# Ranking the norms between sublayers in the scheduler's order, in a decoder layer on one core

## The chip, the cores and the metric

The kernel runs on one core of a Trainium2 chip. The metric is the device time of one execution in microseconds (us). PE is the matrix engine, DVE the vector engine, ACT the scalar engine, POOL GpSimd, and SP the engine whose queue issues most of the transfers.

## The reference, cut to what matters

One decoder layer on x of 512 tokens by 1024 channels in float32. Three sublayers follow each other, and each one is wrapped in two RMS norms, one ahead of it and one behind it:

```python
h = h + 0.5 * rmsnorm(swiglu(rmsnorm(h, ffn1_pre_w), ffn1_w_gu, ffn1_w_down), ffn1_post_w)
u = rmsnorm(h, mix_pre_w)
y = token_mixing(u, mem, w_in, ...)      # HGRN2, dilated attention, attention into memory; gated, then w_out
h = h + rmsnorm(y, mix_post_w)
h = h + 0.5 * rmsnorm(swiglu(rmsnorm(h, ffn2_pre_w), ffn2_w_gu, ffn2_w_down), ffn2_post_w)

def rmsnorm(x, w):
    return x * rsqrt(mean(x * x, axis=-1) + 1e-6) * w
```

The two places where a sublayer's last product, its post norm, the sum into h and the next sublayer's pre norm follow each other are called passages here: passage 1 from the first feed-forward net to the mixing, passage 2 from the mixing to the second net. What follows the last product of the second net is called the tail.

## The kernel before, in words

Every float32 product is made of three products of numbers split into a high and a low part (`split`: ACT rounds the high part, DVE subtracts it from the source; `wsplit` does so for weights). Large products go in pairs of 7 products of quarters (`pair`, `product`), which need sums of quarters of the activations: the tiles t1, t2, t3, t4, made at the end of `prenorm`.

The 512 tokens are four tiles of 128, t = 0 to 3. At the end of `ffn`, a loop over t makes two halves of 512 channels with `down` (12 matmuls a half; the last half of t=3 in two pieces of 256, so that what follows can begin sooner). DVE adds each half from PSUM into y, ACT squares it and sums the squares (`square`, L174), DVE multiplies y by the norm's weights in place, DVE and POOL make the factor r (`rstd`: v on DVE, L180, the power on POOL, L181), and `postnorm` adds y times r to h (L244). `out_proj` does the same with its two halves in two outer rounds, so that only the second one has a norm behind it.

Then `after(h, t)` spills h to DRAM and starts `prenorm` as a task: squares, rstd and the scaled halves u (L190) at once, then, when the planner's clock has gone on by `LAT['norm']` = 8 us, two sets of four transposes on PE (L352) into a bank of the pool px (3 banks), the split into xhi and xlo, and a copy to SBUF (`keep`, L208). For t = 2 and 3 the sums of quarters follow in the same task. The planner only decides where in the written program a task's next part stands; its clock goes on by fixed amounts per matmul.

The written program is then put in order by a scheduler at build time. Each instruction has a number, by its place in the program. For each engine the scheduler issues, among the instructions that it takes to be ready by its own estimate of durations, the one with the lowest number. On the chip each engine then goes through its list in that order, and waits on semaphores for what is not there yet. Tiles of a pool with one tag are given out in the order in which the program writes them first, whatever the numbers. The pool `slots` has 37 tiles of 128x512, and holds y, h, gains, u, scratch of the squares, copies and activations alike. Transfers made with `fetch` stay in written order on SP.

In the program behind the passages stand, at passage 1, `values` for the columns C_HI (weights from `rows`, products of all four t), then the pairs of the first HGRN heads; at passage 2, two plain blocks of the second net (`gu_plain`, first for t = 0 and 1, then for t = 2 and 3; their weights come from `wcol`), then pairs.

Of the kernel before, what the change touches and what calls it, by code (L numbers as in the profile page):

```python
# [1 line left out]

# [10 lines left out]
ALU = mybir.AluOpType  # L13
# [6 lines left out]
NT = T // P  # L20
# [24 lines left out]
CHUNKS2 = (2, 4, 4, 4, 4, 4)  # L45

LAT = dict(comb=1.0, mem0=0.5, mem1=8.0, mem2=1.5, hg=1.5, hgx=6.0, hg1=6.0, hg2=11.0, hg3=6.0, hg4=6.0, dil0=4.0, dil1=17.0, dil2=5.0,
           dil3=3.0, norm=8.0, mnorm=5.0, mload=10.0, start=0.1, step=2.0, keep=2.0)
PLAN = dict(early1=2, plain1=2, early2=2, plain2=2)
HALVES = (slice(0, 512), slice(512, 1024))  # L50


class Layer:
# [3 lines left out]
    def __init__(self, ctx, tc):  # L57
# [30 lines left out]

        self.strict = False

    def spawn(self, gen):
        task = [0.0, gen, False]
        self.tasks.append(task)
        self.advance(task)
        return task

    def advance(self, task):  # L100
        outer, self.polling = self.polling, True
        try:
            task[0] = self.t + next(task[1])
        except StopIteration:
            task[2] = True
            self.tasks.remove(task)
        self.polling = outer

    def tick(self, us):
        self.t += us  # L110
        while not self.polling:
            due = [x for x in self.tasks if x[0] <= self.t]
            if not due:
                break
            self.advance(min(due, key=lambda x: x[0]))
# [83 lines left out]
    def prenorm(self, src, gain, t, lat, raw):  # L199


        nc = self.nc
        ts = slice(t * P, (t + 1) * P)
        pts = []

        def keep(hf):
            raw[t, hf] = self.slot((P, 4, P))
            nc.scalar.copy(raw[t, hf], pts[hf])  # L208

        wait = self.strict and t < 2  # L210
        for x in self.normed(src, gain, lat, self.psum if self.strict and t == 1 else self.paux):
            if isinstance(x, float):
                yield x
                continue
            hf = len(pts)
            pts.append(x)
            self.split(self.xhi[hf][:, :, ts], self.xlo[hf][:, :, ts], x)
            if not wait and (t < 2 or hf == 0):
                keep(hf)
        if wait:  # L220
            def later():
                yield LAT['keep']
                keep(0)
                keep(1)
            self.spawn(later())
        if t < 2:
            return
        ts = slice((t - 2) * P, (t - 1) * P)
        x11, x21, x12 = raw[t - 2, 0], raw[t - 2, 1], raw[t, 0]
        t1, t2, t3 = self.slot((P, 4, P)), self.slot((P, 4, P)), self.slot((P, 4, P))  # L230
        self.tt(t1, x11, x12, ALU.subtract)
        nc.vector.scalar_tensor_tensor(out=t2, in0=t1, scalar=-1.0, in1=pts[1], op0=ALU.mult, op1=ALU.subtract)
        self.tt(t3, x12, pts[1], ALU.subtract)
        for n, x in (("t1", t1), ("t2", t2), ("t3", t3)):
            self.split(self.xc[n][0][:, :, ts], self.xc[n][1][:, :, ts], x)
            yield LAT['comb']
        self.tt(t3, x21, t2, ALU.add)
        self.split(self.xc["t4"][0][:, :, ts], self.xc["t4"][1][:, :, ts], t3)
# [127 lines left out]
    def pair(self, ops):  # L366


        nc = self.nc
        a, cp, cq = self.psum((P, HT)), self.slot(), self.slot()  # L370
        self.product(a, ops, 1)
        nc.scalar.copy(cp[:, :HT], a)
        u, v, p7 = cq[:, :HT], cp[:, HT:], cq[:, HT:]
        b = self.psum((P, HT))
        self.product(b, ops, 6)
        self.tt(u, cp[:, :HT], b, ALU.add)
        c = self.psum((P, HT))
        self.product(c, ops, 5)
        nc.scalar.copy(v, c)  # L379
        d = self.psum((P, HT))  # L380
        self.product(d, ops, 7)
        nc.scalar.copy(p7, d)  # L382
        self.tt(v, p7, v, ALU.subtract)
        self.product(a, ops, 2, False)
        self.product(c, ops, 3, False)
        self.product(d, ops, 4, False)
        return a, u, c, d, v
# [30 lines left out]
            self.mm3(out, (x[k][0][:, ts], x[k][1][:, ts]), w[k], k == 0, k == n - 1)  # L418


    def ffn(self, w_gu, w_down, w_post, ready, reload, after, chunks, early, plain):


        nc = self.nc
        y = [[self.slot() for _ in range(2)] for _ in range(NT)]
# [18 lines left out]
        def gu_plain(w, act, cs):  # L444
            n = cs.stop - cs.start
            pg, pu = self.psum((P, n)), self.psum((P, n))
            self.proj_T(pg, w[0], self.uT, cs)
            self.proj_T(pu, w[1], self.uT, cs)
            sg = self.slot((P, n))
            nc.scalar.activation(sg, pg, AF.Silu)  # L450
            self.tt(sg, sg, pu, ALU.mult)
            self.split(act[0][:, cs], act[1][:, cs], sg)
# [17 lines left out]
        tasks, heads = [ready[0]()], []  # L470
# [10 lines left out]
        for i in range(2):  # L481
            self.need(*tasks[i])
            for w, act in heads:
                gu_plain(w, act, slice(i * HT, (i + 1) * HT))
        f0, before, ws = 0, None, []
        for n in chunks:
            act = []
# [22 lines left out]
        h = reload()  # L510
        gain = self.bcast_gain(w_post)
        tasks = []
        for t in range(NT):
            whole, parts = slice(0, 512), (slice(0, 256), slice(256, 512))
            ss = []
            for hf in range(2):
                for cs in parts if hf == 1 and t == NT - 1 else (whole,):
                    down(t, hf, act, [w[hf] for w in ws], False, self.psum, cs)
                    ss.append(self.square(y[t][hf][:, cs], hf, 0.5))
                    if len(ss) == 3:  # L520
                        self.tt(ss[1], ss[0], ss[1], ALU.add)
                        del ss[0]
            self.tt(y[t][0], y[t][0], gain[0], ALU.mult)
            r = self.rstd(ss, 0.5)
            self.tt(y[t][1], y[t][1], gain[1], ALU.mult)
            self.postnorm(r, y[t], h[t], parts if t == NT - 1 else (whole,))
            tasks.append(self.spawn(after(h, t)))
        return tasks


# [448 lines left out]
    def out_proj(self, z, w_out, w_post, reload, after):  # L979

        nc = self.nc
        y, ss = [[None, None] for _ in range(NT)], [[None, None] for _ in range(NT)]
        tasks = []
        gain = self.bcast_gain(w_post)
        for hf in range(2):
            w = self.rows(w_out, hf * 512, 512)
            if hf == 1:
                h = reload()
            for t in range(NT):
                ps = self.psum()  # L990
                self.proj_N(ps, z, slice(t * P, (t + 1) * P), w)
                ss[t][hf] = self.square(ps, hf, 1.0)
                y[t][hf] = self.slot()
                self.tt(y[t][hf], ps, gain[hf], ALU.mult)
                if hf == 1:
                    self.postnorm(self.rstd(ss[t], 1.0), y[t], h[t])
                    tasks.append(self.spawn(after(h, t)))
        return tasks


# [7 lines left out]
def layer_kernel(ctx, tc, a, nbias, hmask, out):  # L1008
    nc = tc.nc
    L = Layer(ctx, tc)  # L1010
    x = a["x"][0]

    gpre, raw = [], {}
# [27 lines left out]
    def spill(name):  # L1041
        return [[L.dram.tile([P, T], F32, tag=f"{name}{t}{hf}", name=f"{name}{t}{hf}") for hf in range(2)] for t in range(NT)]

    def reload(src):
        def go():
            h = [[L.slot() for _ in range(2)] for _ in range(NT)]
            for t in range(NT):
                for hf in range(2):
                    L.fetch(h[t][hf], src(t, hf))
            return h  # L1050
        return go
# [13 lines left out]
    def store(h, t):  # L1065
        for c, n in ((0, 512), (512, 256), (768, 256)) if t == NT - 1 else ((0, 512), (512, 512)):
# [3 lines left out]
    h1, h2 = spill("h1"), spill("h2")  # L1070
    ready = L.ffn(a["ffn1_w_gu"][0], a["ffn1_w_down"][0], a["ffn1_post_w"][0], [first, second],
                  reload(lambda t, hf: x[t * P:(t + 1) * P, HALVES[hf]]), follow(h1, a["mix_pre_w"][0]), CHUNKS1, PLAN['early1'], PLAN['plain1'])
    z = L.mixing(a, ready, nbias)
    ready = L.out_proj(z, a["w_out"][0], a["mix_post_w"][0], reload(lambda t, hf: h1[t][hf]), follow(h2, a["ffn2_pre_w"][0]))
    L.ffn(a["ffn2_w_gu"][0], a["ffn2_w_down"][0], a["ffn2_post_w"][0], [lambda: ready[:2], lambda: ready[2:]], reload(lambda t, hf: h2[t][hf]), store, CHUNKS2, PLAN['early2'], PLAN['plain2'])


def constants():
# [39 lines left out]
```

## Time and profile before

| | us |
|---|---|
| median of 3 runs | 1367.82 (1366.94 to 1368.05) |
| the profiled execution's own time | 1367.62 |
| its span, first to last instruction | 1365.8 |
| PE busy in the span | 1331.6 |
| DVE busy | 1050.7 |
| ACT busy | 742.2 |
| POOL busy | 107.0 |

The span is 1.82 us shorter than the execution's time. A row of the timeline has the start, the duration, the engine, the line, what is written from what, the number of instructions that were merged, and in brackets the idle time of the engine before it with what ended it. A duration includes some overlap with the next instruction of the same engine: DVE rows of 0.68 us stand 0.60 us apart, matmuls of 512 columns (0.39 us) 0.227 us apart, and those of 256 columns (0.28 us) 0.12 us apart. Passage 1 lies at about 345 to 400 us, passage 2 at 980 to 1030 us, the tail from 1335 us on.

### The profile page before, as it was taken

What the parts mean: (1) busy time and instruction counts of PE and PEld (TensorE: products, weight loads), DVE (VectorE), ACT (ScalarE), POOL (GpSimd) and SP (SyncE); (2) the same over time, 40 slices, a digit from 0 to 9 for tenths busy, and PEclk for the clock granted to TensorE, in tenths of its full rate; (3) what the DMA queues carried; (4) which work ended last, traced back from release to release, by engine and by line L of the source; (5) the groups of instructions that cost most, each with busy time, mean ns of one, the idle gap of its engine ahead of it and who ended that gap; (6) DMA issues with size and microseconds to landing.
All of it is one profiled execution on the core that took longest, in us unless ns stands there. A gap on an engine that the chain in (4) does not pass through costs nothing.

```text
span 1365.8 us, 24324 instructions
## 1 busy us (share of the span) xinstructions
PE 1331.6 (97%) x9197; PEld 1233.0 (90%) x9197; DVE 1050.7 (77%) x1996; ACT 742.2 (54%) x1527; POOL 107.0 (8%) x140
## 2 busy tenths in 40 slices
PE   6999999999999999999999999999999999999997
PEld 6999999999789888899899999999889999999996
DVE  6887776777798975598888988897478877677765
ACT  6665544555467655355554755566366655445541
POOL 1111111110100000000000100000011111111100
PEclk9999999999999999999999999999999999999999
DMA  9676565554435335334224333335465765655513
GB/s 271 141 182 184 148 156 142 143 151 125 168 94 177 96 98 163 123 102 117 63 78 124 100 95 93 108 94 154 135 190 135 186 181 151 152 139 148 146 47 139
DMA packets 238123, 185.76 MB, mean 136 GB/s; under 512 B 9109, under 2 KB 198966, under 8 KB 238006
## 3 DMA queue, kind: packets, MB, share of 16 engines
q1 hardware_dynamic: 224246, 160.02, 39.5%
q0 software_dynamic: 12032, 21.04, 9.4%
q10 hardware_dynamic: 1728, 3.15, 0.6%
q8 instruction: 72, 1.18, 0.3%
q14 instruction: 45, 0.37, 0.1%
HBM read 153.73 MB, written 9.47 MB: 119 GB/s over the span
## 4 chain that ended last, share of the span: by engine, by line
PE 87%; DVE 6%; issue 3%; DMA 2%; ACT 1%; POOL 1%; SPq 0%; POOLq 0%; DVEq 0%; ACTq 0%
PE ps L361 17%; PE ps L363 17%; PE ps L362 17%; PE ps L341 6%; PE ps L342 6%; PE ps L343 6%; PE px L341 5%; PE px L342 5%; PE px L343 5%; PE px L348 4%; DVE s L158 2%; PE px L352 1%; DVE w L158 1%; POOL r L181 1%; DVE s L244 1%
## 5 line engine op out<-in xcount | busy, mean ns | idle before, releaser
L161 ACT ACTIVATE w<-sum 128x512 fp32r<-128x512 f32 x288 | 180.2, 631 | 215.9 <-PE ps L362 180.3
L158 DVE TENSOR_TENSOR w<-sum,w 128x512 fp32r<-128x512 f32 x288 | 196.9, 687 | 76.9 <-ACT w L161 75.9
L361 PE MATMUL ps<-xhi,w 128*128 128x256 f32 x864 | 246.3, 285 | 0.9 <-ACT s L379 0.9
L363 PE MATMUL ps<-xhi,w 128*128 128x256 f32 x864 | 244.8, 283 | 0.0
L362 PE MATMUL ps<-xlo,w 128*128 128x256 f32 x864 | 244.4, 283 | 0.0
L161 ACT ACTIVATE w<-st 128x512 fp32r<-128x512 f32 x260 | 162.9, 630 | 126.7 <-PE ps L362 90.0
L158 DVE TENSOR_TENSOR w<-st,w 128x512 fp32r<-128x512 f32 x260 | 177.2, 688 | 39.3 <-ACT w L161 37.9
L158 DVE TENSOR_TENSOR s<-s,s 128x256 f32<-128x256 f32 (+3 forms) x316 | 176.8, 564 | 16.2 <-ACT s L161 4.6
L361 PEld LDWEIGHTS ps<-xhi,w 128*128 128x128 f32 x864 | 165.6, 192 | 3.8 <-ACT s L379 1.2
L362 PEld LDWEIGHTS ps<-xlo,w 128*128 128x128 f32 x864 | 165.6, 192 | 2.4 <-issue 0.2
L363 PEld LDWEIGHTS ps<-xhi,w 128*128 128x128 f32 x864 | 165.5, 192 | 0.0
L158 DVE TENSOR_TENSOR sum<-sum,st 128x512 f32<-128x512 f32 x176 | 120.4, 687 | 10.9 <-issue 5.0
L158 DVE TENSOR_TENSOR s<-s,ps 128x256 f32<-128x256 f32 (+1 forms) x194 | 92.3, 476 | 29.4 <-PE ps L343 24.0
L341 PE MATMUL px<-s,s 128*128 128x512 f32 x288 | 112.6, 391 | 0.0
L342 PE MATMUL px<-s,s 128*128 128x512 f32 x288 | 112.5, 391 | 0.0
L343 PE MATMUL px<-s,s 128*128 128x512 f32 x288 | 112.0, 389 | 0.0
L361 PE MATMUL ps<-t4hi,w 128*128 128x256 f32 x288 | 81.9, 284 | 0.8 <-ACT s L382 0.8
L361 PE MATMUL ps<-t3hi,w 128*128 128x256 f32 x288 | 82.6, 287 | 0.0
L362 PE MATMUL ps<-t3lo,w 128*128 128x256 f32 x288 | 82.0, 285 | 0.0
L361 PE MATMUL ps<-t1hi,w 128*128 128x256 f32 x288 | 81.7, 284 | 0.0
L363 PE MATMUL ps<-t1hi,w 128*128 128x256 f32 x288 | 81.6, 283 | 0.0
L362 PE MATMUL ps<-t2lo,w 128*128 128x256 f32 x288 | 81.5, 283 | 0.0
(186 smaller groups left out, 3344.2 us busy)
## 6 DMA issues: line engine op xcount, KB each, us to landing
st<-in_ffn_w_gu_dram SPq DMA_DIRECT2D x48, 512.0 KB, 4.9
st<-in_w_in_dram SPq DMA_DIRECT2D x48, 512.0 KB, 3.7
st<-in_ffn_w_down_dram SPq DMA_DIRECT2D x44, 512.0 KB, 3.8
sum<-in_ffn_w_gu_dram SPq DMA_DIRECT2D x80, 256.0 KB, 3.4
sh<-in_ffn_w_gu_dram SPq DMA_DIRECT2D x40, 256.0 KB, 3.8
sum<-sh POOLq DMA_DIRECT2D x40, 256.0 KB, 3.6
sum<-st POOLq DMA_DIRECT2D x40, 256.0 KB, 3.3
sum<-in_w_in_dram SPq DMA_DIRECT2D x32, 256.0 KB, 2.9
```

Source lines behind the costliest of these rows:

```text
L158: self.pin(self.nc.vector.tensor_tensor(out=out, in0=a, in1=b, op=op))
L161: self.pin(self.nc.scalar.activation(hi, src, AF.Copy))
L181: self.nc.gpsimd.tensor_tensor(out=r, in0=v, in1=self.mhalf[:, :1], op=ALU.pow)
L244: self.nc.vector.scalar_tensor_tensor(out=h[hf][:, cs], in0=y[hf][:, cs], scalar=r, in1=h[hf][:, cs], op0=ALU.mult, op1=ALU.add)
L341: mm(out, lhsT=lhs[0], rhs=rhs[0], start=first, stop=False)
L342: mm(out, lhsT=lhs[0], rhs=rhs[1], start=False, stop=False)
L343: mm(out, lhsT=lhs[1], rhs=rhs[0], start=False, stop=last)
L348: self.nc.tensor.matmul(out, lhsT=lhsT, rhs=rhs, start=start, stop=stop, **k)
L352: self.nc.tensor.transpose(out, in_, self.ident)
L361: mm(out, lhsT=lh, rhs=rh, start=first and k == 0, stop=False, skip_group_check=True)
L362: mm(out, lhsT=lh, rhs=rl, start=False, stop=False, skip_group_check=True)
L363: mm(out, lhsT=ll, rhs=rh, start=False, stop=k == 3, skip_group_check=True)
```

## The change

Instructions within `with self.sooner()` get a number lower by 300. These are, at both passages, the squares and the whole norm behind the last product, and all that the `prenorm` tasks issue when they are started or go on (squares, rstd, u, transposes, splits). The adds of `down` into y stay as they were.

Out of `prenorm` come, at both passages, the copies of t = 0 and 1, which a task of normal rank makes 2 us of the planner's clock later, and the sums of quarters (`combine`), which are tasks of normal rank too; `pair` makes sure that they are written before it. The start of the kernel is as before (`apart` is set behind the first net's first blocks).

In the tail (`last`) only the squares have a lower number. The products with the norm's weights go into tiles of their own (z), not in place, and are written behind the last square of their t; for t=3 the second half's product is cut in two pieces.

```diff
+AHEAD = 300
...
+    def spawn(self, gen, urgent=False):
+        task = [0.0, gen, False, urgent]
...
     def advance(self, task):
...
-            task[0] = self.t + next(task[1])
+            with self.sooner() if task[3] else nullcontext():
+                task[0] = self.t + next(task[1])
...
+    def sooner(self):
+        return self.tc.high_priority(offset=AHEAD)
...
     def prenorm(self, src, gain, t, lat, raw):
         wait = self.strict and t < 2
+        behind = not self.strict and self.apart
...
-            if not wait and (t < 2 or hf == 0):
+            if not wait and (t < 2 and not behind or t >= 2 and hf == 0):
                 keep(hf)
-        if wait:
+        if wait or behind and t < 2:
             def later():
                 yield LAT['keep']
                 keep(0)
                 keep(1)
             self.spawn(later())
         if t < 2:
             return
+        if behind:
+            def later():
+                yield LAT['comb']
+                yield from self.combine(raw, pts[1], t)
+            self.combs.append(self.spawn(later()))
+        else:
+            yield from self.combine(raw, pts[1], t)
...
     def pair(self, ops):
+        self.need(*self.combs)
+        self.combs = []
...
     def ffn(..., plain, last=False):
...
+        self.apart = True
         f0, before, ws = 0, None, []
...
                     down(t, hf, act, [w[hf] for w in ws], False, self.psum, cs)
-                    ss.append(self.square(y[t][hf][:, cs], hf, 0.5))
-                    if len(ss) == 3:
-                        self.tt(ss[1], ss[0], ss[1], ALU.add)
-                        del ss[0]
-            self.tt(y[t][0], y[t][0], gain[0], ALU.mult)
-            r = self.rstd(ss, 0.5)
-            self.tt(y[t][1], y[t][1], gain[1], ALU.mult)
-            self.postnorm(r, y[t], h[t], parts if t == NT - 1 else (whole,))
-            tasks.append(self.spawn(after(h, t)))
+                    with self.sooner():
+                        ss.append(self.square(y[t][hf][:, cs], hf, 0.5))
+                        if len(ss) == 3:
+                            self.tt(ss[1], ss[0], ss[1], ALU.add)
+                            del ss[0]
+            if last:
+                z = [self.slot() for _ in range(2)]
+                for hf in range(2):
+                    for cs in parts if hf == 1 and t == NT - 1 else (whole,):
+                        self.tt(z[hf][:, cs], y[t][hf][:, cs], gain[hf][:, cs], ALU.mult)
+                self.postnorm(self.rstd(ss, 0.5), z, h[t], parts if t == NT - 1 else (whole,))
+                after(h, t)
+                continue
+            with self.sooner():
+                self.tt(y[t][0], y[t][0], gain[0], ALU.mult)
+                r = self.rstd(ss, 0.5)
+                self.tt(y[t][1], y[t][1], gain[1], ALU.mult)
+                self.postnorm(r, y[t], h[t], parts if t == NT - 1 else (whole,))
+            tasks.append(self.spawn(after(h, t), True))
...
     def out_proj(...):
-                ss[t][hf] = self.square(ps, hf, 1.0)
-                y[t][hf] = self.slot()
-                self.tt(y[t][hf], ps, gain[hf], ALU.mult)
+                with self.sooner() if hf == 1 else nullcontext():
+                    ss[t][hf] = self.square(ps, hf, 1.0)
+                    y[t][hf] = self.slot()
+                    self.tt(y[t][hf], ps, gain[hf], ALU.mult)
+                    if hf == 1:
+                        self.postnorm(self.rstd(ss[t], 1.0), y[t], h[t])
                 if hf == 1:
-                    self.postnorm(self.rstd(ss[t], 1.0), y[t], h[t])
-                    tasks.append(self.spawn(after(h, t)))
+                    tasks.append(self.spawn(after(h, t), True))
```

The second call of `ffn` gets `last` = True.

More of the change, by code (lines that the diff above doesn't have):

```diff
@@ L1 @@
-from contextlib import ExitStack
+from contextlib import ExitStack, nullcontext
 import concourse.bass as bass
@@ L89, in __init__ @@
         self.strict = False
-    def spawn(self, gen):
-        task = [0.0, gen, False]
+        self.apart, self.combs = False, []
+    def spawn(self, gen, urgent=False):
+        task = [0.0, gen, False, urgent]
         self.tasks.append(task)
@@ L227, in prenorm, with combine @@
             return
+        if behind:
[5 more added lines that the diff above has]
+            yield from self.combine(raw, pts[1], t)
+    def combine(self, raw, x22, t):
+        nc = self.nc
         ts = slice((t - 2) * P, (t - 1) * P)
@@ L231, in prenorm @@
         self.tt(t1, x11, x12, ALU.subtract)
-        nc.vector.scalar_tensor_tensor(out=t2, in0=t1, scalar=-1.0, in1=pts[1], op0=ALU.mult, op1=ALU.subtract)
-        self.tt(t3, x12, pts[1], ALU.subtract)
+        nc.vector.scalar_tensor_tensor(out=t2, in0=t1, scalar=-1.0, in1=x22, op0=ALU.mult, op1=ALU.subtract)
+        self.tt(t3, x12, x22, ALU.subtract)
         for n, x in (("t1", t1), ("t2", t2), ("t3", t3)):
@@ L418, in proj_N, with ffn @@
             self.mm3(out, (x[k][0][:, ts], x[k][1][:, ts]), w[k], k == 0, k == n - 1)
-    def ffn(self, w_gu, w_down, w_post, ready, reload, after, chunks, early, plain):
+    def ffn(self, w_gu, w_down, w_post, ready, reload, after, chunks, early, plain, last=False):
         nc = self.nc
@@ L1074, in layer_kernel @@
     ready = L.out_proj(z, a["w_out"][0], a["mix_post_w"][0], reload(lambda t, hf: h1[t][hf]), follow(h2, a["ffn2_pre_w"][0]))
-    L.ffn(a["ffn2_w_gu"][0], a["ffn2_w_down"][0], a["ffn2_post_w"][0], [lambda: ready[:2], lambda: ready[2:]], reload(lambda t, hf: h2[t][hf]), store, CHUNKS2, PLAN['early2'], PLAN['plain2'])
+    L.ffn(a["ffn2_w_gu"][0], a["ffn2_w_down"][0], a["ffn2_post_w"][0], [lambda: ready[:2], lambda: ready[2:]], reload(lambda t, hf: h2[t][hf]), store, CHUNKS2, PLAN['early2'], PLAN['plain2'], True)
 def constants():
```

## The prediction

> **What bounds the kernel now.** I read the page's head and its chain first, then the waits of PE in the stretches that the change touches, then the timelines of those stretches.
>
> ```profile
> span 1365.8 us, 24324 instructions
> PE 1331.6 (97%) x9197; PEld 1233.0 (90%) x9197; DVE 1050.7 (77%) x1996; ACT 742.2 (54%) x1527; POOL 107.0 (8%) x140
> PE 87%; DVE 6%; issue 3%; DMA 2%; ACT 1%; POOL 1%; SPq 0%; POOLq 0%; DVEq 0%; ACTq 0%
> ```
>
> PE bounds the kernel: it is idle for 1365.8 - 1331.6 = 34.2 us only, and the chain that ended last is 87% PE. A change of order takes no matmul away, so it can only win idle time of PE or lose more of it. The waits of PE, passage 1 first and passage 2 behind it, and how busy the engines are there:
>
> ```profile
> PE px L352 <- DVE s L190: 1.9, 2, 1.1
> PE ps L342 <- DVE w L158: 1.8, 1, 1.8
> ...
> PE ps L342 <- DVE xlo L158: 1.9, 1, 1.9
> PE px L352 <- DVE s L190: 0.8, 1, 0.8
> ...
> 360.00:380.00 20.00, 17.43 (x97) 14.03 (x96) 18.14 (x36) 12.09 (x31) 3.69 (x5) 1.00 0.24 79
> 380.00:400.00 20.00, 18.79 (x93) 15.53 (x94) 19.56 (x35) 14.51 (x29) 1.45 (x3) 1.00 0.30 93
> 1000.00:1020.00 20.00, 17.22 (x119) 15.37 (x118) 17.14 (x32) 13.87 (x34) 5.41 (x7) 1.00 0.55 166
> ```
>
> The columns of a wait are the total, the number and the longest in us; those of a stretch are its length and the busy time of PE, PE's weight loads, DVE, ACT and POOL. So passage 1 can give at most 1.9 + 1.8 = 3.7 us and passage 2 at most 1.9 + 0.8 = 2.7 us. In both DVE is nearly full (18.14 and 19.56 of 20 us in passage 1), which matters below. The tail comes on top.
>
> **The tail.** This is the one part whose mechanism does not hang on ranks.
>
> ```profile
> 1356.52 0.28 PE L343 MATMUL ps<-s,s 128*128 128x256 f32 x1
> ...
> 1350.52 0.68 DVE L158 TENSOR_TENSOR s<-s,ps 128x512 f32<-128x512 f32 x1
> 1351.98 0.69 DVE L158 TENSOR_TENSOR s<-s,s 128x512 f32<-128x512 f32 x1 [0.79 <-ACT s L174]
> 1356.66 1.01 DVE L158 TENSOR_TENSOR s<-s,ps 128x512 f32<-128x512 f32 x2
> 1358.13 0.69 DVE L158 TENSOR_TENSOR s<-s,s 128x512 f32<-128x512 f32 x1 [0.46 <-ACT s L174]
> 1358.74 0.41 DVE L158 TENSOR_TENSOR s<-s,ps 128x256 f32<-128x256 f32 x1
> 1359.07 0.15 DVE L158 TENSOR_TENSOR ss<-ss,ss 128x1 f32<-128x1 f32 x1
> 1359.79 0.21 DVE L180 TENSOR_SCALAR v<-ss,ss 128x1 f32<-128x1 f32 x1 [0.57 <-ACT s L174]
> 1359.92 0.68 DVE L158 TENSOR_TENSOR s<-s,s 128x512 f32<-128x512 f32 x1
> ...
> 1359.24 0.42 ACT L174 ACTIVATE s<-s 128x256 f32<-128x256 f32 x1 [0.75 <-DVE ss L158]
> ...
> 1342.21 0.56 POOL L181 TENSOR_TENSOR r<-v,mhalf 128x1 f32<-128x1 f32 x1 [56.36 <-DVE v L180]
> 1360.14 0.86 POOL L181 TENSOR_TENSOR r<-v,mhalf 128x1 f32<-128x1 f32 x1 [4.86 <-DVE v L180]
> ```
>
> The last matmul ends at 1356.52 + 0.28 = 1356.80, but the add of its piece into y starts at 1358.74, 1.94 us later. In between stands the product of y's first half with the weights (1358.13): it is made in place, so it has waited 0.46 us for ACT to have squared the same half, and on an engine that works in order the add has waited behind it. The same wait is seen in the tile before (0.79 us ahead of 1351.98). Tile by tile DVE takes 6.14 us (1350.52 to 1356.66), and PE's 24 matmuls take 24 x 0.227 = 5.45 us, so DVE falls behind. With z no product waits for a square. DVE's period falls to 6.14 - 0.79 = 5.35 us, below PE's, so it stands ready for the last piece.
>
> New sum from the last matmul's end: the add at 1356.86, 0.33 us (1358.74 to 1359.07); the sum of the squares' sums 0.15; then, as their tiles are given out behind that of the last square, the three pieces of z, 0.61 (1358.13 to 1358.74) + 2 x 0.33 = 1.27. So v starts at 1356.86 + 0.33 + 0.15 + 1.27 = 1358.6 instead of 1359.79: 1.2 us won. ACT's square (0.42 us and its read-out) runs beside the products. What follows v is the same three instructions of L244, but the product that stood behind v (1359.92) is gone.
>
> That gives one more term. POOL's power takes 0.86 us where DVE runs a product of two SBUF tiles beside it (1360.14), and 0.56 us where it does not (1342.21). It would now be alone: 0.3 us more, so 1.5 us for the tail. The Trainium skill ("SBUF — State Buffer", "SBUF: two separate sides") says that a DVE instruction with two SBUF inputs and a GpSimd instruction lock each other out of a shared pair of ports for a whole instruction. By that rule the 0.3 us are a wait for DVE, which agrees with the two rows; a rule of free sharing would give 1.2 us.
>
> Bounds: if v is put ahead of the products, 1.27 us more are won and the 0.3 us lost, but the square then bounds, 1356.86 + 0.33 + 0.72 (1359.07 to 1359.79) = 1357.91, which is 1.9 us in all. If a first product still stands ahead of the add, 0.61 of the 1.2 us go: 0.6 us. I take 1.5, since it follows the written order.
>
> **Passage 2.**
>
> ```profile
> 994.71 1.41 DVE L190 SCALAR_TENSOR_TENSOR s<-s,r,s 128x512 f32<-128x512 f32 x2 [1.74 <-DMA s<-in_ffn_pre_w_dram]
> 1005.14 0.68 DVE L158 TENSOR_TENSOR w<-st,w 128x512 fp32r<-128x512 f32 x1
> 1007.59 1.28 DVE L158 TENSOR_TENSOR xlo<-px,xhi 128x512 fp32r<-128x512 f32 x2
> ...
> 1003.68 0.60 ACT L174 ACTIVATE s<-ps 128x512 f32<-128x512 f32 x1
> 1004.27 1.15 ACT L161 ACTIVATE w<-st 128x512 fp32r<-128x512 f32 x2
> 1005.31 1.08 ACT L161 ACTIVATE xhi<-px 128x512 fp32r<-128x512 f32 x2
> 1009.86 0.61 ACT L174 ACTIVATE s<-ps 128x512 f32<-128x512 f32 x1
> ...
> 996.85 1.03 PE L352 MATMUL px<-ident,s 128*128 128x128 f32 x8
> 1002.51 1.03 PE L352 MATMUL px<-ident,s 128*128 128x128 f32 x8
> 1006.13 0.28 PE L341 MATMUL ps<-xhi,w 128*128 128x256 f32 x1
> 1008.33 0.39 PE L342 MATMUL ps<-xlo,w 128*128 128x256 f32 x1 [1.92 <-DVE xlo L158]
> 1018.81 0.63 PE L352 MATMUL px<-ident,s 128*128 128x128 f32 x4 [0.83 <-DVE s L190]
> ```
>
> The transposes of t=1 are done at 1002.51 + 1.03 = 1003.5. ACT then squares (1003.68), rounds two weight pieces (1004.27 to 1005.31), and only then rounds xhi. PE has begun its block at 1006.13 and waits 1.92 us for xlo. Ranked ahead of the weights, xhi is at 1004.27 and xlo from about 1004.9, two times 0.60, so it is there at 1006.1: the 1.92 us go. What is late next is the weight: two roundings of xhi (1.04 us) put the low weight piece of 1005.14 to about 1006.2 at the earliest, behind scalings of the norm. PE has a first quarter of the block to do before it needs that piece, 12 matmuls x 0.12 = 1.44 us, to 1007.6. I put 0.6 us of new wait there, one DVE instruction.
>
> The last matmuls of t=3 end near 1006.1, but its square runs at 1009.86, behind copies and weights that were written earlier. With rank it comes up to 3.7 us sooner, so the 0.83 us ahead of the transposes at 1018.81 go.
>
> Against this: the transposes get rank as well. They now stand 8 us of the planner's clock behind the norm's start, and were in place or late by little. With rank they go into PE's list as soon as the scheduler takes u to be ready, and PE works in order. At 996.85 the first half of u has been done since 994.71 + 0.7 = 995.4, so pulling these transposes forward by more than 1.4 us makes PE wait; u itself was late there for the gain's transfer (1.74 us). An early wait takes some of the later ones with it. I charge 0.8 us, the nearest seen wait of transposes here (0.83); the ends are 0 and 3 us, four transposes each as late.
>
> Sum of passage 2: -1.9 - 0.8 + 0.6 + 0.8 = -1.3 us, ends -2.7 and +1.
>
> **Passage 1.**
>
> ```profile
> 367.08 0.66 PE L352 MATMUL px<-ident,s 128*128 128x128 f32 x4 [1.13 <-DVE s L190]
> 381.11 0.50 PE L342 MATMUL ps<-w,xhi 128*128 128x512 f32 x1 [1.78 <-DVE w L158]
> ...
> 378.91 1.54 DVE L244 SCALAR_TENSOR_TENSOR s<-s,r,s 128x512 f32<-128x512 f32 x3 [0.44 <-POOL r L181]
> 380.37 0.68 DVE L158 TENSOR_TENSOR w<-st,w 128x512 fp32r<-128x512 f32 x1
> 380.98 0.68 DVE L158 TENSOR_TENSOR xlo<-px,xhi 128x512 fp32r<-128x512 f32 x1
> ```
>
> Here the norm is already ahead: the piece of weights that PE waits for (380.37) stands behind the scalings of t=3 (378.91), so rank does not move them. What rank moves is xlo of t=2 (380.98), which comes ahead of that piece. That delays the weight by 0.6 us, but gives PE a third tile for the weights that it has. I count half of the 1.78 us as won, -0.9. The waits of the transposes (1.9 us) depend on when u is ready; I count them nearly whole, -0.1. Copies and sums of quarters leave the ranked tasks, which costs nothing as long as the first pair starts behind them. Sum: -1.0 us, ends -3.7 (all of it) and +1.7 (four transposes pulled forward by the 1.13 us that one shows now, less the 1.9 and the weight's 0.9).
>
> **Sum.** -1.5 - 1.3 - 1.0 = -3.8 us. From the profiled execution's 1367.62 us that is 1363.8. The median of the runs lies 0.2 us above that execution, so 1364.0 us.
>
> **The rivals.**
>
> The waits only move. DVE is full through passage 1, and rank gives it no time; tiles of the 37 slots are given out in written order whatever the rank, so squares may stay where they are, and the ranks do little of what they say. Then only the tail is left, -1.5 us: 1366.3. For it: 19.56 of 20 us. Against it: ACT has room (13.87 of 20), and the 1.92 us come from ACT's order.
>
> Transposes too early. If the scheduler's estimate of the norm is short, all eight sets stand in PE's list ahead of their u. If each waits 1.13 us, as the worst does now, that is 9.0 us, less the 1.9 + 0.8 us they cost now, less 1.92 and 1.5 us as above: +2.9, so 1370.7 us. It decides from about 0.8 us a set on, where it eats the whole gain. For it: two sets of passage 1 already are late though written 8 us behind. Against it: a PE that waits early reaches the later waits later. A later copy also holds px's three banks longer, which works the other way, since it keeps transposes back.
>
> All of it: both passages' waits gone and 1.9 us in the tail, -3.7 - 2.7 - 1.9 = -8.3: 1359.5 us. For it nothing but the order; against it DVE's load.
>
> **How the numbers follow.** About 0.2%, 2.7 us, is what a measurement of this kernel can tell from no change, so the edge of faster is 1365.1 us. The forecast has 0.50, and its own range of 1362 to 1366 lies with 0.42 below the edge. All of it has 0.10, waits that only move 0.23, all within the edge but for little. Early transposes have 0.17. So faster 0.52, same 0.30, slower 0.18. For 8 in 10 the range reaches two thirds of the way from the forecast to both outer cases (1359.5 and 1370.7): 1361.0 to 1368.5 us.
>
> **What would show it.** In the tail the last piece's add within 0.3 us of the last matmul, the products between it and v, and POOL's last power at 0.56 us. In passage 2 xhi of t=1 ahead of the two weight roundings, no wait for xlo of 1.9 us, and the square of t=3 within 1 us of its matmuls. In passage 1 the wait for a weight at half or less. Wrong would be: waits of transposes on u of more than 4 us in sum over both passages, new waits for weights in their place, or an unmoved last add.

## The result and the profile after

The changed kernel takes 1385.22 us (median of 4 runs, 1383.20 to 1385.25) against 1367.93 us of the kernel before on the same chip: a ratio of 1.0123, 95% interval 1.0106 to 1.0140, 17.3 us slower. The prediction was 1364.0 us, faster. It was wrong in sign.

The profiled execution after took 1385.25 us. The page's head:

```profile
span 1383.5 us, 24339 instructions
PE 1336.7 (97%) x9197; PEld 1235.6 (89%) x9197; DVE 1052.8 (76%) x1997; ACT 744.8 (54%) x1527; POOL 105.0 (8%) x140
```

The work is the same (9197 matmuls, DVE and ACT within 3 us of before). The span is 17.7 us longer: PE is idle for 1383.5 - 1336.7 = 46.8 us instead of 34.2, which is 12.6 us, and busy for 5.1 us more with the same matmuls. The idle time lies at the passages and behind the second one, as the waits show; the busy time is taken up in the last section. The waits of PE in the kernel after, at passage 1, then at passage 2, then behind it at the first pair:

```profile
PE px L373 <- ACT s L216: 5.5, 1, 5.5
PE px L373 <- DVE s L198: 3.7, 3, 1.7
...
PE px L373 <- DVE s L198: 2.6, 4, 0.7
PE px L373 <- ACT s L216: 2.0, 1, 2.0
PE ps L362 <- DVE s L166: 1.8, 1, 1.8
...
PE ps L382 <- ACT s L395: 2.4, 1, 2.4
```

And the stretches of the kernel after, with the granted clock ahead of the last two columns:

```profile
380.00:400.00 20.00, 13.50 (x61) 10.98 (x62) 13.68 (x26) 11.49 (x29) 3.40 (x6) 0.83 0.17 64
1020.00:1040.00 20.00, 14.65 (x99) 13.18 (x100) 14.14 (x25) 11.79 (x27) 3.08 (x5) 0.91 0.39 106
1080.00:1100.00 20.00, 17.56 (x124) 16.87 (x123) 14.95 (x28) 13.48 (x28) 1.75 (x2) 0.91 0.67 160
```

The waits for weights and xlo of before are gone or small. What is new is that transposes (L373, L352 before) wait for copies (L216, the `keep` of before's L208) and longer for u (L198, L190 before); at passage 2 a product also waits 1.8 us for an add of DVE (L166). And DVE, which was full in passage 1 (19.56 of 20 us at 380 to 400), is now busy for 13.68 us there: nothing was crowded, something came late. What came late is seen in the timeline of passage 1, PE first, then DVE and ACT:

```profile
359.95 0.66 PE L373 MATMUL px<-ident,s 128*128 128x128 f32 x4 [1.67 <-DVE s L198]
360.36 0.48 PE L362 MATMUL ps<-w,s 128*128 128x512 f32 x1
361.47 0.28 PE L363 MATMUL ps<-w,s 128*128 128x256 f32 x1
364.22 0.40 PE L362 MATMUL ps<-w,xhi 128*128 128x512 f32 x1
378.15 0.39 PE L362 MATMUL ps<-s,s 128*128 128x512 f32 x1
384.51 0.69 PE L373 MATMUL px<-ident,s 128*128 128x128 f32 x2 [5.52 <-ACT s L216]
...
363.59 0.41 DVE L166 TENSOR_TENSOR s<-s,ps 128x256 f32<-128x256 f32 x1
365.18 0.41 DVE L166 TENSOR_TENSOR s<-s,ps 128x256 f32<-128x256 f32 x1
374.53 0.68 DVE L166 TENSOR_TENSOR s<-s,ps 128x512 f32<-128x512 f32 x1
379.03 0.69 DVE L166 TENSOR_TENSOR s<-s,ps 128x512 f32<-128x512 f32 x1
...
379.75 0.63 ACT L182 ACTIVATE s<-s 128x512 f32<-128x512 f32 x1 [1.49 <-DVE s L166]
383.89 1.05 ACT L216 COPY s<-px 128x512 f32<-128x512 f32 x2
```

The rows of 256 columns are the two last pieces of t=3. They were written last, and are now done first, at 361.5 to 364.1. At 364.22 the mixing's `values` begin (xhi). The second half of t=2, of which PE made one matmul at 360.36, is made bit by bit between those of `values`, and its last group of three begins at 378.15; DVE adds it at 379.03, behind both pieces of t=3 and its first half (374.53). So the norm of t=2 begins some 14 us behind t=3's last piece, ACT's list has its squares (379.75) ahead of the copies of t=0 and 1 (383.89), and transposes stand in PE's list that need a bank of px from these copies.

The order of PE is turned round, and not only for what was ranked: the products of `down` have no rank, nor has `values`. The reason is in the two lines of `advance`. The guard lowers the counter from which instructions get their numbers by 300, and puts it back when the `with` block ends. But a task's last step ends by the exception StopIteration, which leaves the block, and on this way the counter isn't put back. Read while the program is written, the counter falls at eight places, by about 287 numbers each, and stays low behind each.

These are the ends of the four norm tasks of each passage. At passage 1 the first lies in the second half of t=2, behind its first three matmuls; the second lies ahead of the two pieces of t=3, and the other two lie in `values`. What is written later so gets lower numbers than what is still to be done, and the scheduler issues it first. That is theory A. Theory B is what the new wait names: the copies, which the change writes 2 us of the planner's clock later, hold the three banks of px.

In the tail the change did what it is for:

```profile
1375.45 0.28 PE L364 MATMUL ps<-s,s 128*128 128x256 f32 x1
...
1376.12 0.16 DVE L166 TENSOR_TENSOR ss<-ss,ss 128x1 f32<-128x1 f32 x1 [0.85 <-ACT s L182]
1376.20 0.42 DVE L166 TENSOR_TENSOR s<-s,ps 128x256 f32<-128x256 f32 x1
1376.53 1.35 DVE L166 TENSOR_TENSOR s<-s,s 128x512 f32<-128x512 f32 x3
1377.80 0.21 DVE L188 TENSOR_SCALAR v<-ss,ss 128x1 f32<-128x1 f32 x1
1378.74 1.54 DVE L265 SCALAR_TENSOR_TENSOR s<-s,r,s 128x512 f32<-128x512 f32 x3 [0.73 <-POOL r L189]
```

From the end of the last matmul (1375.73) to the first scaling (1378.74) there are 3.01 us; before, the first scaling stood here, and there were 1361.04 - 1356.80 = 4.24:

```profile
1361.04 1.54 DVE L244 SCALAR_TENSOR_TENSOR s<-s,r,s 128x512 f32<-128x512 f32 x3 [0.44 <-POOL r L181]
```

### The profile page after: what moved, and what is told of

It is laid out like the page before. It is cut to its first block, busy times and chain, and to the rows that moved or that the text cites. A ratio compares the mean times of both kernels' runs of the same rounds, so it can differ in the third digit from the quotient of the medians.

```text
span 1383.5 us, 24339 instructions
## 1 busy us (share of the span) xinstructions
PE 1336.7 (97%) x9197; PEld 1235.6 (89%) x9197; DVE 1052.8 (76%) x1997; ACT 744.8 (54%) x1527; POOL 105.0 (8%) x140
## 4 chain that ended last, share of the span: by engine, by line
PE 47%; DVE 3%; DMA 2%; ACT 1%; issue 1%; POOL 0%; SPq 0%; DVEq 0%; POOLq 0%; ACTq 0%
PE ps L384 9%; PE ps L382 9%; PE ps L383 9%; PE ps L363 3%; PE ps L362 3%; PE ps L364 3%; PE px L369 2%; PE px L362 2%; PE px L363 2%; PE px L364 2%; PE px L373 1%; DVE w L166 1%; DVE s L166 1%; ACT s L182 0%; DMA sum<-sh 0%
## 5 line engine op out<-in xcount | busy, mean ns | idle before, releaser
L166 DVE TENSOR_TENSOR w<-sum,w 128x512 fp32r<-128x512 f32 x288 | 197.4, 688 | 77.3 <-ACT w L169 76.0
L166 DVE TENSOR_TENSOR w<-st,w 128x512 fp32r<-128x512 f32 x260 | 177.2, 689 | 44.8 <-ACT w L169 42.5
L166 DVE TENSOR_TENSOR s<-s,s 128x256 f32<-128x256 f32 (+3 forms) x317 | 176.8, 564 | 14.3 <-ACT s L169 4.6
L166 DVE TENSOR_TENSOR sum<-sum,st 128x512 f32<-128x512 f32 x176 | 120.6, 688 | 16.9 <-issue 4.9
L166 DVE TENSOR_TENSOR s<-s,ps 128x256 f32<-128x256 f32 (+1 forms) x194 | 92.4, 477 | 28.2 <-PE ps L364 22.6
L382 PE MATMUL ps<-t4hi,w 128*128 128x256 f32 x288 | 82.1, 285 | 0.8 <-ACT s L405 0.8
L382 PE MATMUL ps<-t1hi,w 128*128 128x256 f32 x288 | 81.8, 284 | 0.0
L383 PE MATMUL ps<-t4lo,w 128*128 128x256 f32 x288 | 81.7, 284 | 0.0
L384 PE MATMUL ps<-t4hi,w 128*128 128x256 f32 x288 | 81.6, 283 | 0.0
```

Source lines behind the costliest of these rows:

```text
L166: self.pin(self.nc.vector.tensor_tensor(out=out, in0=a, in1=b, op=op))
L382: mm(out, lhsT=lh, rhs=rh, start=first and k == 0, stop=False, skip_group_check=True)
L383: mm(out, lhsT=lh, rhs=rl, start=False, stop=False, skip_group_check=True)
L384: mm(out, lhsT=ll, rhs=rh, start=False, stop=k == 3, skip_group_check=True)
```

## The experiments

All times are compared with the kernel before on the same chip, where it had a median of 1368.8 to 1369.1 us; gains in us are the ratio's part of that. Lines move by a few from kernel to kernel.

**restored: the changed kernel with the counter put back.**

```diff
             with self.sooner() if task[3] else nullcontext():
-                task[0] = self.t + next(task[1])
+                step = next(task[1], None)
+            if step is None:
+                raise StopIteration
+            task[0] = self.t + step
```

> The changed kernel, but a ranked task takes its last step in such a way that the number counter goes back up when the task has ended. In the kernel after, the counter is lowered by 300 for a ranked step and put back behind it, except where the step is the task's last: the task then ends by an exception, and the counter stays low, so all that is written later starts about 287 numbers lower. It happens eight times, at each end of a norm task. Theory A (the counter that stays low makes later work overtake the rest of the down products): the loss goes, 1364 us (1361 to 1370), no wait of transposes for the copies over 1 us, and the second half of t=2 is added before the pieces of t=3. Theory B (the copies written 2 us later hold the three banks of px): the copies stand where they stand after, so it stays at 1378 or more, with the 5.5 us wait for a copy.

Measured: 1367.52 us, ratio 0.9992 (0.9977 to 1.0006). The loss is gone. Its waits of PE at passage 1 and at passage 2:

```profile
PE ps L366 <- DVE w L169: 1.5, 2, 1.0
PE px L376 <- DVE s L201: 1.0, 3, 0.6
...
PE px L376 <- DVE s L201: 3.2, 3, 1.3
PE ps L367 <- DVE w L169: 0.8, 1, 0.8
```

No transpose waits for a copy, though the copies are written where they are in the kernel after. Theory B falls. The time lies in the upper part of the range that was expected, and its interval holds 1: the ranks as meant bring little or nothing.

**lowered: the kernel before, with nothing but the fall of the counter.**

```diff
         except StopIteration:
             task[2] = True
             self.tasks.remove(task)
+            if self.apart and task[3]:      # the norm tasks of both passages
+                try:
+                    with self.tc.high_priority(offset=290):
+                        raise StopIteration
+                except StopIteration:
+                    pass
```

> The kernel before, nothing ranked and nothing moved, but the number counter is lowered by 290 for good at each of the eight ends of a norm task at the two passages. Theory A: this alone makes the loss, 1378 us or more (before 1367.9), with long waits of PE at both passages. Theory B: copies and sums stand as before, so within 3 us of before, under 1371.

Measured: 1393.61 us, ratio 1.0175 (1.0150 to 1.0200), 24 us slower. The fall alone makes more than the whole loss, with nothing ranked, moved or changed in the tail. The loss needn't be of one size with that of the kernel after: in the kernel before, the sums of quarters end the tasks of t=2 and 3, so these falls come later in the program. At passage 1 PE now waits for sums of quarters and for xlo:

```profile
PE ps L368 <- ACT t2hi L168: 3.8, 1, 3.8
PE ps L350 <- DVE xlo L165: 3.1, 1, 3.1
PE ps L369 <- DVE t1lo L165: 2.6, 1, 2.6
```

**inplace: the changed kernel, copies and sums back in the norm task, the counter still falling.**

```diff
-        behind = not self.strict and self.apart
+        behind = False
```

> The changed kernel with copies and sums of quarters back in the norm task, as before; ranks, the low counter and the tail stay. Theory A: 1378 us or more. Theory B: the banks are free as early as before, the wait for a copy goes, 1372 us or less.

Measured: 1390.50 us, ratio 1.0152 (1.0127 to 1.0176), no faster than the kernel after (1.0106 to 1.0140). The waits for copies are gone, as theory B wanted, and the time with them is not: transposes wait for u instead, 9.2 us at passage 1 and 9.3 at passage 2.

```profile
PE px L373 <- DVE s L198: 9.2, 2, 7.2
PE ps L364 <- DVE xlo L166: 2.0, 2, 1.8
...
PE px L373 <- DVE s L198: 9.3, 4, 4.6
```

So the name in the wait was only what came last; behind both names stands the norm that began late.

**lowered75: as lowered, a fall of 75 instead of 290.**

```diff
-                    with self.tc.high_priority(offset=290):
+                    with self.tc.high_priority(offset=75):
```

> As the run lowered, with 75 instead of 290 numbers lost at each of the eight ends. Theory A: only what was written within the last 75 numbers can be overtaken, so part of the 25 us is left, 1371 to 1385. Rival: any fall of the counter does it whatever its size, 1390 or more.

Measured: 1381.74 us, ratio 1.0093 (1.0079 to 1.0108), 13 us slower: about half of lowered's loss for a quarter of the fall. The size matters, as theory A says.

**second: put back at passage 1, falling at passage 2.** The tasks of `out_proj` get a mark 2; the lines shown are against restored.

```diff
-                step = next(task[1], None)
+                step = next(task[1]) if task[3] == 2 else next(task[1], None)
```

> The changed kernel with the counter put back at the four ends of passage 1, and left low at the four ends of passage 2. Between the two traces the kernel after falls back by about 8 us up to 420 us of the span, by 7 more over passage 2, and by 4 at 1075 to 1095 us, where a pair waits for a load (sh) issued late. Theory A: passage 2's four falls cost 7 + 4 by themselves, the late load among them, so 11 us over restored, 1378 us. Rival (the falls of passage 1 carry over, as they leave the transfers in another order): 1372 or less, or 1383 and more.

Measured: 1374.71 us, ratio 1.0049 (1.0030 to 1.0067), 0.57% or 7.8 us above restored, 5 to 11 by the two intervals. The median lies between the two expectations. It fits the 7 us of passage 2 without the 4 us behind it, and the trace says the same: the first pair waits 1.2 us there instead of 2.4, and the clock of 1080 to 1100 us is at 1.00. So passage 2's falls cost about 8 us by themselves. The late load that the expectation speaks of needs those of passage 1 too, or both orders together; which, stays open.

**tail: the kernel before with the change in the tail alone** (the block under `if last:`, nothing ranked).

> The kernel before with the change in the tail alone: products with the norm's weights in tiles of their own, behind the last square of their t. Both theories: the tail wins 1.2 us as the two traces show (last matmul to the first scaling 4.24 us before, 3.01 after), so 1366.7 us against 1367.9. As nothing is ranked, the add of the square sums may stand behind the last add of y, which would give 0.3 us more: 1366.4.

Measured: 1367.82 us, ratio 0.9995 (0.9982 to 1.0008). In its trace the last matmul ends at 1357.35 and the first scaling starts at 1360.36: 3.01 us, as after. So 1.2 us are shown by the trace, and the time can't tell them from nothing. Without rank, too, the sum of the square sums stands ahead of the last add and waits 0.85 us for ACT, so the 0.3 us more didn't come.

**whole: as restored, with copies and sums of quarters in the ranked tasks** (`behind = False` in restored).

> As the run restored, with the copies and the sums of quarters back in the ranked tasks. With the counter put back, theory A leaves these moves a small part: the sums (some nine instructions of DVE of 0.6 us for t=2 and t=3 each) now stand ahead of the weights' low pieces, so up to 3 us worse than restored, 1368 to 1371. Theory B, that written place of the copies is what matters, would make it faster than restored.

Measured: 1366.55 us, ratio 0.9990 (0.9979 to 1.0001). No slower than restored, against the expectation, and not clearly faster, as theory B would have it. At passage 1 and passage 2 PE waits 4.0 us in sum, where restored has 6.5 and before 6.4:

```profile
PE px L376 <- DVE s L201: 2.0, 4, 0.8
...
PE px L376 <- DVE s L201: 1.3, 2, 0.7
PE ps L365 <- ACT s L476: 0.7, 1, 0.7
```

All waits for weights, xhi and xlo are gone there. Whether that is worth time, the ratios of restored and whole don't separate.

**late: as restored, transposes at their normal number.** Only a task's first step and the splits are ranked.

```diff
                 step = next(task[1], None)
+            task[3] = False
...
-            self.split(self.xhi[hf][:, :, ts], self.xlo[hf][:, :, ts], x)
+            with self.sooner() if behind else nullcontext():
+                self.split(self.xhi[hf][:, :, ts], self.xlo[hf][:, :, ts], x)
```

> As the run restored (counter put back at each task's end), but only the first step of a norm task (squares, factor, scaled halves) and the splits into xhi and xlo are ranked; the transposes keep their normal number. Restored has 6.5 us of waits of PE in both passages (2.5 and 4.0), as many as before (6.4): the transposes' 0.83 us in passage 2 became 3.2. Theory: that is what ate the gain, so the transposes' waits in passage 2 fall back to 1 us or less, while the wait for xlo stays away, and the time is 1 to 2 us under restored, 1366 against 1367.5. Rival (rank gains nothing at all, the waits only move): other waits take the place, 1367 to 1368.

Measured: 1369.78 us, ratio 1.0007 (0.9989 to 1.0025): no gain. At passage 2:

```profile
PE px L378 <- DVE s L202: 2.1, 2, 1.7
PE ps L367 <- ACT xhi L173: 1.6, 1, 1.6
```

The transposes still wait 2.1 us, and xhi is now what PE waits for. The rival was right: the wait moved.

**best: as late, and the tail with its last add free.**

```diff
                         if len(ss) == 3:
-                            self.tt(ss[1], ss[0], ss[1], ALU.add)
-                            del ss[0]
+                            self.tt(ss[2], ss[1], ss[2], ALU.add)
+                            del ss[1]
             if last:
+                r = self.rstd(ss, 0.5)
                 z = [self.slot() for _ in range(2)]
...
-                self.postnorm(self.rstd(ss, 0.5), z, h[t], parts if t == NT - 1 else (whole,))
+                self.postnorm(r, z, h[t], parts if t == NT - 1 else (whole,))
```

> As the run late, and in the tail the sum of two square sums takes the two pieces of the second half, so that it can't stand ahead of the last add, and the factor is written ahead of the weight products. In the tail of restored DVE waits 0.85 us for ACT with that sum ahead of the last add. Last add at once after the last matmul (within 0.1 us instead of 0.5), v after the first two products, the power beside the third: from the last matmul to the first scaling 2.3 us instead of 3.0, so 0.7 us under late, 1365.3.

Measured: 1368.87 us, ratio 1.0006 (0.9991 to 1.0021). In the time no gain shows; in the trace it does. Last matmul, then DVE:

```profile
1360.08 0.28 PE L369 MATMUL ps<-s,s 128*128 128x256 f32 x1
...
1360.40 0.42 DVE L170 TENSOR_TENSOR s<-s,ps 128x256 f32<-128x256 f32 x1 [0.50 <-PE ps L369]
...
1361.80 0.21 DVE L192 TENSOR_SCALAR v<-ss,ss 128x1 f32<-128x1 f32 x1
1361.93 0.42 DVE L170 TENSOR_TENSOR s<-s,s 128x256 f32<-128x256 f32 x1
1362.79 1.54 DVE L270 SCALAR_TENSOR_TENSOR s<-s,r,s 128x512 f32<-128x512 f32 x3 [0.44 <-POOL r L193]
```

DVE stands ready and the add follows the last matmul by 0.04 us. From there to the first scaling it is 2.43 us, 1.8 less than before.

**tail2: the kernel before with this tail alone; whole_tail: whole with this tail; whole_tail100: the same with ranks of 100.**

> The kernel before with the tail of best alone, nothing ranked: the passages as before (waits of PE 6.4 us), from the last matmul to the first scaling 2.4 us in place of 4.24, -1.8 us against before.

> The ranks with the counter put back, copies and sums of quarters in the ranked tasks (as in whole), and the tail of best. Both passages had 4.0 us of waits of PE in whole against 6.4 before, and the tail from the last matmul to the first scaling 2.43 us in best against 4.24. Theory: the two add up, -2.4 - 1.8 = -4.2 us against before. Rival: the 2.4 us of whole are a lucky order that the other tail's build doesn't repeat; then -1.8 us alone.

> As whole_tail with ranks of 100 in place of 300. If a rank need only overtake what was written in the last microseconds (a half of t is 15 to 22 numbers long), 100 gives the same order where it counts: within 1 us of whole_tail. If the weights written far ahead must be passed, the waits for xlo and xhi come back, up to 2 us slower.

| | median, us | ratio to before | interval |
|---|---|---|---|
| tail2 | 1366.50 | 0.9982 | 0.9972 to 0.9993 |
| whole_tail | 1365.07 | 0.9977 | 0.9965 to 0.9990 |
| whole_tail100 | 1365.29 | 0.9978 | 0.9967 to 0.9990 |

All three beat both kernels. The tail alone is worth 0.18% (2.5 us, 1.0 to 3.8; 1.8 expected); its trace also has 0.9 us less of a wait for a weight at passage 1 than before, which nothing in its edit aims at. The ranks, put right, add 0.05% by the ratios, which their intervals don't tell from nothing, though the short waits of whole come again (1.8 + 1.7 + 0.7 = 4.2 us in whole_tail). A rank of 100 measures the same as 300.

## Why the prediction was wrong

**The first step failed, one that the prediction took for granted.** It read `sooner` as "a number lower by 300" for what stands in the block, and costed only what ranked instructions pass or push back. It never asked what the counter does behind the block when a task ends. Its rival for a change that doesn't do what it says ("the waits only move") let the ranks do less than meant, not the reverse of it to the rest of the program. The falls cost 1.0123 against 0.9992, 1.3% or some 18 us: about 8 of them at passage 2 (second), the rest of the way at passage 1 and in what both leave behind.

**What the prediction looked at** can be judged by restored, where the ranks do what it assumed.

- The tail: mechanism right, -1.2 us (4.24 to 3.01) where it said -1.5. The products stand between the add and v, and POOL's last power took 0.55 us (1359.50 in restored), as said. What was mis-sized is the add: 0.47 us behind the last matmul, not 0.06, since the sum of the square sums was put ahead of it and waits 0.85 us for ACT.
- Passage 2: the 1.9 us wait for xlo went, as said, and the new wait for a weight is 0.8 us (0.6 said). The transposes are the term that was mis-sized: 3.2 us of waits where the sum left 0.8 (the 0.8 of before taken off, 0.8 charged), a little beyond the charge's outer end of 3 us. Passage 2 costs 4.0 us of waits instead of 2.7, +1.3 where it said -1.3.
- Passage 1: 2.5 us of waits instead of 3.7, -1.2 where it said -1.0, but otherwise shared out: the weight gave 0.3 of its 1.8 us (0.9 said), the transposes 0.9 of their 1.9 (0.1 said).
- The sum of these is -1.1 us where -3.8 was said, and restored measures 0.08% less, 1.1 us, with an interval that holds zero. "Transposes too early" had its place and its cause right at passage 2 (1.25 us ahead of t=0's, where u waits 2.13 us for the transfer of the norm's weights), at about half its price: 4.2 us of such waits in both passages, not 9.0.
- "Copies and sums of quarters leave the ranked tasks, which costs nothing as long as the first pair starts behind them": in the traces it costs 2.5 us of waits (restored 6.5, whole 4.0), in the time nothing that can be told. "A later copy also holds px's three banks longer, which works the other way": the bank did hold the transposes back, 5.5 us in the kernel after, and that was a loss. It came of the copies' place behind a late norm in ACT's list, and without the fall of the counter it isn't there.

A row of the tail was read wrongly. The prediction has the 0.56 us power of 1342.21 with no product beside it, but one did run there in the kernel before:

```profile
1342.30 0.69 DVE L158 TENSOR_TENSOR s<-s,s 128x512 f32<-128x512 f32 x1 [0.23 <-DVE v L180]
```

It began 0.09 us behind the power, where the product of 1359.92 began 0.22 us ahead of the 0.86 us power of 1360.14. So the two rows differ in which began first. That the power takes 0.55 us alone is shown by restored.

**The signs** that it named were the right ones for another reason: it had waits of transposes on u of more than 4 us in sum as what would show it wrong, and in the kernel after there are 3.7 + 2.6 on u and 5.5 + 2.0 on copies. It expected them as the price of rank. Restored shows that price: 1.0 + 3.2 = 4.2 us on u, so the sign is met there too, by little, and no loss of time shows. What the kernel after has beyond it, the 7.5 us on copies above all, is the price of an order that nobody wrote.

## What to carry to other kernels

Where a change ranks instructions for a scheduler, print the number of every instruction as it is written, or at least look for a place where the numbers go back: a guard around a step that can end by an exception is one. When an engine waits for something new after a change of order, and the engine that it waits for is less busy than before (DVE 13.68 of 20 us where it had 19.56), look for work that was put behind later work, and not at the instruction that the wait names; here copies, u, xlo and sums of quarters took turns in that name. And a pipeline's end is worth a look by itself: products in tiles of their own, one sum of two numbers taken from other operands, and v ahead of the last product gave all of the gain that the times can show.

## What the runs showed of the hardware that was not expected

PE's 5.1 us of additional busy time are not more work: the granted clock was 0.83 at 380 to 400 us, behind the 5.5 us wait, and 0.91 at 1020 to 1040 and 1080 to 1100; before, it was 1.00 in all of them. In stretches of 1 us the clock reads 1.00 or 0.50, and a value between only where it changes. It was at 0.50 from 382.0 to 388.8 us, and for 3.4 us in each of the other two. An estimate, PE's busy time in these stretches times what was missing of the clock, gives 5.2 us for the three; another 3.4 us at 16 to 20 us of the span, far from the passages, would give 1.7 more, so the estimate is somewhat high.

The stretch of 380 to 400 us in inplace, where PE waited 7.2 us at once, at 0.66:

```profile
380.00:400.00 20.00, 11.02 (x38) 8.29 (x37) 12.88 (x24) 9.76 (x25) 3.40 (x6) 0.66 0.22 78
```

And a stretch of restored at 0.92, with no single wait over 1.4 us:

```profile
1000.00:1020.00 20.00, 17.83 (x118) 16.53 (x117) 16.19 (x28) 12.95 (x29) 3.69 (x6) 0.92 0.51 148
```

So on top of 12.6 us of added idle time come 5.1 us of slower matmuls. The Trainium skill ("TensorE: Matmul & The Clock Gate", Part 1) has a clock that goes to half after an idle window of about 3.4 us, and back after about as much work. An estimate by these figures: the 5.5 us wait would have 2.1 + 3.4 us at half speed, which makes 0.86 over 20 us, and 0.83 was measured; the 7.2 us wait would give 0.82, and 0.66 was measured. So the direction agrees, and the size only for the first. In inplace a second wait of 1.75 us, up to 393.63, fell into the low time, which this estimate leaves out, and the clock came back only at 399.7 us.

An idle stretch of 3.4 us isn't needed for a fall, though. In restored the clock was at 0.50 from 1017.0 to 1020.4 us, and ahead of that stood a wait of 0.83 us, matmuls, and part of one of 1.34 us. In the kernel after it fell at about 1085.1 us, some 1.6 us behind the end of the 2.44 us wait (1083.57). How much idle time brings a fall, no run here shows.
